# Two hybrid decoder layers on one core: the order of issue taken from the scheduler's time-line simulator

## The chip, the cores and the metric

The kernel runs on one core of one Trainium2 chip. The metric is the device time of one execution in microseconds. Every time below comes from one profiled execution of the kernel before, unless it is called a median of runs. The engines are TensorE (PE; PEld is its loading of weights), VectorE (DVE), ScalarE (ACT), GpSimd (POOL) and SyncE (SP); SP issues the DMAs.

## The reference, cut to what matters

One sequence of 256 rows of 2048 numbers goes through two layers. Each layer has an attention part (eight forgetting heads and eight differential heads) and an MLP part (hidden width 8192), and both are modulated by vectors that come from the condition `c` through the large matrix `w_ada` (2048 by 12288 for each layer).

```python
c_act = jax.nn.silu(c)
for l in range(DEPTH):                                   # 2 layers
    mod = c_act @ w_ada[l] + b_ada[l]
    sh_a, sc_a, g_a, sh_m, sc_m, g_m = jnp.split(mod[:, None, :], 6, axis=-1)
    h = x * (1.0 + sc_a) + sh_a
    y = _mixer(h, cos, sin, w_in[l], b_f[l], ..., w_o[l], _lambda_init(l))
    x = _layernorm(ALPHA * x + (1.0 + g_a) * y, ln1_g[l], ln1_b[l])
    h = x * (1.0 + sc_m) + sh_m
    y = jnp.square(jax.nn.relu(h @ w_up[l])) @ w_down[l]
    x = _layernorm(ALPHA * x + (1.0 + g_m) * y, ln2_g[l], ln2_b[l])
return x
```

All weights are float32: 768 blocks of 512 KB for the projections and 384 blocks of 512 KB for `w_ada`.

## The kernel before, in words

**One projection block.** A block is a 128x1024 piece of a weight matrix. SP loads it into a tile `raw` (L141). ACT copies it to `wh`, its rounded high part (L135), and DVE subtracts to get `wl`, the low part (L136). PE then multiplies in three products, high by high, high by low and low by high, with the activations `hT`, which were split in the same way (L485 is the high part, L486 the low part). A block is 12 matmuls of 128x512 (L302 to L304, in `mm3`) or 24 of 128x256 (L328 to L331, in `proj_T`). There are 7 buffers for `raw`, and 3 each for `wh` and `wl`: PE can be at most three blocks behind ACT and DVE.

**The modulation.** The product of `c` with `w_ada` is done on DVE. SP loads a block `rawa` (L156) into the same 7 buffers that `raw` uses, and DVE adds the block, times one column of `c`, to `acc` (L147 for the first block, L149 for the 15 that follow). Sixteen blocks make one piece of a modulation vector: PE transposes `acc` (L166), DVE reduces it (L171) and adds the bias `badaT` (L125, L173). ACT and DVE make `hT` from it (L483 to L486). For the two gates, the `acc` that comes out is split like a weight (its `wh` and `wl` take two of the projection's buffers) and goes through PE once with a matrix of ones (L201, L202).

**Stages.** The first layer's input projection is done in four passes over a quarter of the input columns each, since a pass can start as soon as its quarter of the modulation is there: piece 0 before the first matmul, the others beside the matmuls of the pass before. The passes end at about 96, 156, 215 and 300 us. The heads (softmax L597, gather of the gate biases `FR` L846), the output projection (`w_o`, added to the rows `xacc` at L495 to L498), a layer norm (statistics L502 to L506, normalized at L511, transposed at L470, its scale and shift applied later at L545 and L546 with the rows `gb` and `bb`) and the MLP follow, and then the second layer.

**What sets the order.** Every engine executes its instructions in a fixed order and waits at the first that isn't ready. The program is written with an interleaving of its own: `block` is called for each weight block and, by counters, mixes in blocks of `w_ada` (`side`), steps of the heads (`tasks`), and pieces of the layer norm's scale and shift (`later`); the numbers AHEAD, HOLDS, WAIT, GAP, LATER, PREP, STEP and RATES at its head set how much comes when. The layer in which the kernel is written takes the program and orders the instructions of every engine and the DMAs with a scheduler, which simulates the program as it goes; buffers are given out along that simulated run, and waits follow from it. In the listings, names carry a number: `rawa_1045` is the buffer that the program asked for as its 1045th object, and `wl_1004` is the low part made from `raw_1001` and `wh_1003`.

## Time and profile before

| what | value |
|---|---|
| median of 3 runs | 2357.38 us (2354.28 to 2359.78) |
| the profiled execution | 2353.96 us |
| its span in the profile | 2352.2 us |
| PE busy, share of the span | 2278.0 us, 97% |
| PE's weight loads (PEld) | 1958.9 us, 83% |
| DVE busy | 1791.8 us, 76% |
| ACT busy | 1156.4 us, 49% |
| moved by DMA | 619.36 MB, mean 263 GB/s |

The span is the time between the first and the last event of the profile; 1.8 us of the execution lie around it. A share of busy time is a mean over the whole span. A row of the time line tells the start, the duration, the engine, the line and the operation, and in brackets how long the engine stood idle just before and what ended this.

### The profile page before, as it was taken

What the parts mean: (1) busy time and instruction counts of PE and PEld (TensorE: products, weight loads), DVE (VectorE), ACT (ScalarE), POOL (GpSimd) and SP (SyncE); (2) the same over time, 40 slices, a digit from 0 to 9 for tenths busy, and PEclk for the clock granted to TensorE, in tenths of its full rate; (3) what the DMA queues carried; (4) which work ended last, traced back from release to release, by engine and by line L of the source; (5) the groups of instructions that cost most, each with busy time, mean ns of one, the idle gap of its engine ahead of it and who ended that gap; (6) DMA issues with size and microseconds to landing.
All of it is one profiled execution on the core that took longest, in us unless ns stands there. A gap on an engine that the chain in (4) does not pass through costs nothing.

```text
span 2352.2 us, 33293 instructions
## 1 busy us (share of the span) xinstructions
PE 2278.0 (97%) x12444; PEld 1958.9 (83%) x12444; DVE 1791.8 (76%) x2339; ACT 1156.4 (49%) x1684; POOL 35.1 (1%) x60
## 2 busy tenths in 40 slices
PE   4999999899999999999999999999999999999998
PEld 3878798799989888888877779987888888888886
DVE  7899988989888777888777975777675666555657
ACT  3544675345546345346444664544544643643542
POOL 0000010000000000000000000000000000000000
PEclk9999999999999999999999999999999999999999
DMA  9998578888898888888759867764687677655553
GB/s 341 329 331 310 199 272 307 316 313 327 303 351 299 307 283 305 316 285 307 274 189 314 293 225 243 254 206 169 226 271 242 232 243 240 229 194 190 186 189 123
DMA packets 174978, 619.36 MB, mean 263 GB/s; under 512 B 20105, under 2 KB 21209, under 8 KB 174817
## 3 DMA queue, kind: packets, MB, share of 16 engines
q1 hardware_dynamic: 174816, 617.25, 75.5%
q8 instruction: 97, 1.59, 0.3%
q14 instruction: 65, 0.52, 0.1%
HBM read 615.07 MB, written 2.10 MB: 262 GB/s over the span
## 4 chain that ended last, share of the span: by engine, by line
PE 85%; DVE 7%; DMA 4%; issue 2%; ACT 2%; POOL 0%; SPq 0%; DVEq 0%; ACTq 0%; POOLq 0%
PE mm L303 15%; PE mm L302 15%; PE mm L304 15%; PE mm L907 7%; PE bank L907 7%; PE mm L331 5%; PE mm L330 5%; PE mm L328 5%; PE mm L909 4%; PE bank L909 4%; DVE wl L136 2%; DVE acc L149 2%; DMA raw<-in_w_in_dram 1%; DMA rawa<-in_w_ada_G_dram 1%; DMA rawa<-in_w_ada_T_dram 1%
## 5 line engine op out<-in xcount | busy, mean ns | idle before, releaser
L135 ACT CAST wh<-raw 128x1024 fp32r<-128x1024 f32 x752 | 789.9, 1051 | 920.6 <-PE mm L304 489.7
L136 DVE TENSOR_TENSOR wl<-raw,wh 128x1024 fp32r<-128x1024 f32 x752 | 914.8, 1222 | 350.4 <-ACT wh L135 348.1
L149 DVE SCALAR_TENSOR_TENSOR acc<-rawa,cact,acc 128x1024 f32<-128x1024 f32 x368 | 471.2, 1280 | 118.8 <-DMA rawa<-in_w_ada_T_dram 66.8
L303 PE MATMUL mm<-wl,Hs 128*128 128x512 f32 x992 | 386.1, 389 | 1.0 <-DVE wl L136 1.0
L302 PE MATMUL mm<-wh,Hs 128*128 128x512 f32 x992 | 386.2, 389 | 0.0
L304 PE MATMUL mm<-wh,Hs 128*128 128x512 f32 x992 | 386.0, 389 | 0.0
L328 PE MATMUL mm<-hT,wh 128*128 128x256 f32 x1024 | 290.3, 284 | 1.9 <-DVE hT L485 1.1
L331 PE MATMUL mm<-hT,wl 128*128 128x256 f32 x1024 | 288.6, 284 | 2.9 <-DVE wl L136 2.4
L330 PE MATMUL mm<-hT,wh 128*128 128x256 f32 x1024 | 289.1, 283 | 0.2 <-DVE hT L486 0.2
L907 PE MATMUL mm<-hT,wh 128*128 128x512 f32 x768 | 287.1, 396 | 0.5 <-DVE hT L486 0.5
L907 PE MATMUL bank<-hT,wh 128*128 128x512 f32 x768 | 286.5, 395 | 0.0
L303 PEld LDWEIGHTS mm<-wl,Hs 128*128 128x128 f32 x992 | 186.2, 188 | 39.7 <-DVE wl L136 1.4
L302 PEld LDWEIGHTS mm<-wh,Hs 128*128 128x128 f32 x992 | 186.2, 188 | 38.8
L304 PEld LDWEIGHTS mm<-wh,Hs 128*128 128x128 f32 x992 | 186.2, 188 | 38.6
L909 PE MATMUL mm<-hT,wl 128*128 128x256 f32 x768 | 215.7, 281 | 0.1
L909 PE MATMUL bank<-hT,wl 128*128 128x256 f32 x768 | 215.4, 280 | 0.0
L302 PE MATMUL mm<-wh,hT 128*128 128x512 f32 x512 | 201.2, 400 | 5.7 <-DVE hT L485 5.7
L303 PE MATMUL mm<-wl,hT 128*128 128x512 f32 x512 | 203.5, 398 | 1.2 <-DVE wl L136 1.0
L304 PE MATMUL mm<-wh,hT 128*128 128x512 f32 x512 | 200.8, 393 | 0.0
L331 PEld LDWEIGHTS mm<-hT,wl 128*128 128x128 f32 x1024 | 195.3, 192 | 5.0 <-DVE wl L136 4.6
L328 PEld LDWEIGHTS mm<-hT,wh 128*128 128x128 f32 x1024 | 196.3, 192 | 3.4 <-DVE hT L485 1.3
L330 PEld LDWEIGHTS mm<-hT,wh 128*128 128x128 f32 x1024 | 196.3, 192 | 0.7 <-DVE hT L486 0.4
(248 smaller groups left out, 2666.6 us busy)
## 6 DMA issues: line engine op xcount, KB each, us to landing
rawa<-in_w_ada_T_dram SPq DMA_DIRECT2D x256, 512.0 KB, 5.2
raw<-in_w_up_dram SPq DMA_DIRECT2D x256, 512.0 KB, 4.7
raw<-in_w_down_dram SPq DMA_DIRECT2D x256, 512.0 KB, 4.5
raw<-in_w_in_dram SPq DMA_DIRECT2D x192, 512.0 KB, 4.8
rawa<-in_w_ada_G_dram SPq DMA_DIRECT2D x128, 512.0 KB, 5.0
raw<-in_w_o_dram SPq DMA_DIRECT2D x64, 512.0 KB, 4.6
gb<-in_ln_g_dram SPq DMA_DIRECT2D x12, 256.0 KB, 5.7
bb<-in_ln_b_dram SPq DMA_DIRECT2D x12, 256.0 KB, 5.2
```

The source lines that it names most:

```text
L135: nc.scalar.copy(wh, raw)
L136: nc.vector.tensor_sub(wl, raw, wh.bitcast(F32))
L149: nc.vector.scalar_tensor_tensor(acc, raw, k, acc, ALU.mult, ALU.add)
L302: nc.tensor.matmul(o, lhsT=hi, rhs=wh, start=start, stop=False)
L303: nc.tensor.matmul(o, lhsT=hi, rhs=wl, start=False, stop=False)
L304: nc.tensor.matmul(o, lhsT=lo, rhs=wh, start=False, stop=stop)
L328: nc.tensor.matmul(o, lhsT=wh[:, j, cs], rhs=hT[:, kt, 0, :], start=first and kt == kt0 and f % 2 == 0, stop=False)
L330: nc.tensor.matmul(o, lhsT=wh[:, j, cs], rhs=hT[:, kt, 1, :], start=False, stop=False)
L331: nc.tensor.matmul(o, lhsT=wl[:, j, cs], rhs=hT[:, kt, 0, :], start=False, stop=last and kt == kt1 - 1 and f % 2 == 1)
L907: nc.tensor.matmul(pu[f], lhsT=wh[:, j, cs], rhs=hT[:, kt].rearrange("p a s -> p (a s)"), start=kt == kt0, stop=False)
L909: nc.tensor.matmul(pu[f][:, 0:S], lhsT=wl[:, j, cs], rhs=hT[:, kt, 0, :], start=False, stop=kt == kt1 - 1)
```

## The change

One line of `kernel` changes:

```diff
-    with tile.TileContext(nc) as tc:
+    with tile.TileContext(nc, schedule_with_timeline_sim=True) as tc:
```

The scheduler has two simulators by which it orders the program. The other one, which is used now, follows a time line of engines and DMA queues. No instruction is added or taken away, none has another shape, and no count of buffers changes: each engine has the same work in another order, and the waits follow from that order. Three places show the kind of move.

On SP's queue at the start of the program (`-` before, `+` after; `xacc` are rows of the input, `pos_i`, `r`, `bfb`, `ta`, `tb` and `subg` are small constants):

```order
 L121 DMA r_119<-in_b_ada_dram 96x128
-L156 DMA rawa<-in_w_ada_T_dram 128x1024 x13
-L141 DMA raw<-in_w_in_dram 128x1024
+L156 DMA rawa<-in_w_ada_T_dram 128x1024 x5
+L1014 DMA xacc<-in_x_dram 128x512
+L156 DMA rawa<-in_w_ada_T_dram 128x1024
+L1014 DMA xacc<-in_x_dram 128x512
+L396 DMA pos_i<-in_positions_dram 128x2x1
+L156 DMA rawa<-in_w_ada_T_dram 128x1024
+L429 DMA r_518<-in_ln_g_dram 32x128
+L429 DMA r_518<-in_ln_b_dram 32x128
+L429 DMA r_518<-in_ln_g_dram 32x128
```

The list goes on in this way until the 16th `rawa`: all six remaining loads of input rows (256 KB each) and 12 loads of constants now stand ahead of or between the first 16 blocks of `w_ada`, where before all of them came later, spread over the passes.

On DVE at the start of the second pass, the kernel before:

```order
L485 CAST hT_102<-h32_806 128x2x256
L486 TENSOR_TENSOR hT_102<-h32_806,hT_102 128x2x256
L485 CAST hT_102<-h32_816 128x2x256
L486 TENSOR_TENSOR hT_102<-h32_816,hT_102 128x2x256
L136 TENSOR_TENSOR wl_876<-raw_873,wh_875 128x1024
L149 SCALAR_TENSOR_TENSOR acc_854<-rawa_906,cact_82,acc_854 128x1024
L136 TENSOR_TENSOR wl_912<-raw_909,wh_911 128x1024
L149 SCALAR_TENSOR_TENSOR acc_854<-rawa_939,cact_82,acc_854 128x1024
L136 TENSOR_TENSOR wl_945<-raw_942,wh_944 128x1024
L149 SCALAR_TENSOR_TENSOR acc_854<-rawa_977,cact_82,acc_854 128x1024
L136 TENSOR_TENSOR wl_983<-raw_980,wh_982 128x1024
L149 SCALAR_TENSOR_TENSOR acc_854<-rawa_998,cact_82,acc_854 128x1024
```

and the changed kernel:

```order
L136 TENSOR_TENSOR wl_912<-raw_909,wh_911 128x1024
L149 SCALAR_TENSOR_TENSOR acc_854<-rawa_939,cact_82,acc_854 128x1024
L485 CAST hT_102<-h32_806 128x2x256
L485 CAST hT_102<-h32_816 128x2x256
L149 SCALAR_TENSOR_TENSOR acc_854<-rawa_977,cact_82,acc_854 128x1024
L486 TENSOR_TENSOR hT_102<-h32_806,hT_102 128x2x256
L486 TENSOR_TENSOR hT_102<-h32_816,hT_102 128x2x256
L149 SCALAR_TENSOR_TENSOR acc_854<-rawa_998,cact_82,acc_854 128x1024
L149 SCALAR_TENSOR_TENSOR acc_854<-rawa_1023,cact_82,acc_854 128x1024
L149 SCALAR_TENSOR_TENSOR acc_854<-rawa_1045,cact_82,acc_854 128x1024
L149 SCALAR_TENSOR_TENSOR acc_854<-rawa_1070,cact_82,acc_854 128x1024
L136 TENSOR_TENSOR wl_945<-raw_942,wh_944 128x1024
```

Blocks 873 and 909 are now split before `hT` is made, and five `acc` steps stand ahead of `wl_945`, where before `wl` and `acc` took turns. In the changed order the load of `rawa_1045` waits for the `acc` step of `rawa_977`, and the load of `rawa_1070` for that of `rawa_1023`, because they get the buffers that these set free.

On DVE in the attention of the first layer, between two weight splits of the output projection, the kernel before:

```order
L136 TENSOR_TENSOR wl_3818<-raw_3815,wh_3817 128x1024
L149 SCALAR_TENSOR_TENSOR acc_3841<-rawa_3911,cact_82,acc_3841 128x1024
L597 ISA s_3791,mn_3792<-bank_3786,mask_89 128x128
L597 ISA mn_3792 128x1
L597 ISA s_3799,mn_3800<-bank_3786,mask_89 128x256
L597 ISA mn_3800 128x1
L136 TENSOR_TENSOR wl_3848<-raw_3845,wh_3847 128x1024
```

and the changed kernel, the first 12 of the 26 rows from the one split to the other:

```order
L136 TENSOR_TENSOR wl_3818<-raw_3815,wh_3817 128x1024
L597 ISA s_3030,mn_3031<-bank_3025,mask_89 128x128
L597 ISA mn_3031 128x1
L597 ISA s_3039,mn_3040<-bank_3024,mask_89 128x128
L597 ISA mn_3040 128x1
L597 ISA s_3047,mn_3048<-bank_3025,mask_89 128x256
L597 ISA mn_3048 128x1
L597 ISA s_3056,mn_3057<-bank_3024,mask_89 128x256
L597 ISA mn_3057 128x1
L846 TENSOR_TENSOR FR_3742<-FG_93,sel_91 128x1024
L149 SCALAR_TENSOR_TENSOR acc_3841<-rawa_3964,cact_82,acc_3841 128x1024
L680 SCALAR_TENSOR_TENSOR MXd_2161<-bank_3151,subg_99,MXd_2161 128x256
```

The softmax rows have lower numbers than the weights beside them: on every engine the weight blocks of the output projection now run ahead of the heads that the program had put before them. In the same way the 16 steps of the first layer norm's scale and shift (L545, L546), with the eight loads of `gb` and `bb`, now stand between `wl_6492` and `wl_6654` (about 622 to 640 us of the profile before) where they stood spread over 673 to 705 us; and on PE the matmuls of one gate half (L201, L202, the first layer's attention gate, half 0) come after 17 blocks that they stood ahead of, so that the gate's `wh` and `wl` are held all that time.

## Rows read from the trace of the kernel before

**Rows 1.** The page's first part: busy time, share of the span, instructions.

```profile
PE 2278.0 (97%) x12444; PEld 1958.9 (83%) x12444; DVE 1791.8 (76%) x2339; ACT 1156.4 (49%) x1684; POOL 35.1 (1%) x60
```

**Rows 2.** PE's waits: operation, what it waited for, total us, times, longest.

```profile
PE bank L166 <- DVE acc L149: 18.4, 1, 18.4
PE bank L470 <- DVE xacc L511: 15.0, 4, 6.9
PE bank L123 <- DMA r<-in_b_ada_dram: 8.0, 1, 8.0
PE mm L302 <- DVE hT L485: 5.7, 3, 3.4
PE mm L303 <- DVE wl L136: 3.1, 4, 1.0
```

**Rows 3.** Groups of the page: line, operation, count, busy us, mean ns, idle before.

```profile
L136 DVE TENSOR_TENSOR wl<-raw,wh 128x1024 fp32r<-128x1024 f32 x752 | 914.8, 1222 | 350.4 <-ACT wh L135 348.1
L149 DVE SCALAR_TENSOR_TENSOR acc<-rawa,cact,acc 128x1024 f32<-128x1024 f32 x368 | 471.2, 1280 | 118.8 <-DMA rawa<-in_w_ada_T_dram 66.8
```

**Rows 4.** Time line of the start: start us, us, engine, line, operation.

```profile
4.16 18.09 SPq L156 DMA_DIRECT2D rawa<-in_w_ada_T_dram  x13
...
11.19 0.26 DVE L125 COPY badaT<-bank 128x96 f32<-128x96 f32 x1 [5.61 <-PE bank L123]
11.37 19.77 DVE L149 SCALAR_TENSOR_TENSOR acc<-rawa,cact,acc 128x1024 f32<-128x1024 f32 x15
...
36.67 0.80 PE L302 MATMUL mm<-wh,hT 128*128 128x512 f32 x1 [3.45 <-DVE hT L485]
```

**Rows 5.** Stretches: us, busy PE, PEld, DVE, ACT, POOL, PE's clock, DMA share, GB/s.

```profile
0.00:36.00 36.00, 4.33 (x18) 3.48 (x18) 23.98 (x25) 5.58 (x8) 4.08 (x28) 1.00 0.95 362
96.00:156.00 60.00, 58.53 (x306) 48.87 (x304) 53.95 (x58) 26.47 (x32) 0.00 (x0) 1.00 0.91 330
464.50:474.50 10.00, 5.36 (x25) 4.97 (x25) 8.72 (x18) 1.93 (x4) 3.04 (x2) 0.50 0.57 189
620.00:640.00 20.00, 20.00 (x90) 16.57 (x89) 15.71 (x15) 10.31 (x13) 0.00 (x0) 1.00 0.90 303
673.00:706.00 33.00, 33.00 (x147) 27.36 (x146) 30.42 (x35) 14.18 (x15) 0.00 (x0) 1.00 0.97 353
1205.00:1208.00 3.00, 3.00 (x16) 2.91 (x15) 2.60 (x7) 2.80 (x7) 0.00 (x0) 0.53 0.00 0
```

**Rows 6.** DMA issues: operation, count, KB each, median us from issue to landing.

```profile
rawa<-in_w_ada_T_dram SPq DMA_DIRECT2D x256, 512.0 KB, 5.2
```

**Rows 7.** SP's time line, second pass: the load of `rawa_1045`.

```profile
105.80 0.33 SPq L156 DMA_DIRECT2D rawa<-in_w_ada_T_dram  x1
```

**Rows 8.** DVE's time line there: `wl_912`, `wl_945`, and the `acc` of `rawa_1045`.

```profile
101.16 1.22 DVE L136 TENSOR_TENSOR wl<-raw,wh 128x1024 fp32r<-128x1024 f32 x1
...
104.55 1.23 DVE L136 TENSOR_TENSOR wl<-raw,wh 128x1024 fp32r<-128x1024 f32 x1 [0.98 <-ACT wh L135]
...
115.74 1.28 DVE L149 SCALAR_TENSOR_TENSOR acc<-rawa,cact,acc 128x1024 f32<-128x1024 f32 x1
```

**Rows 9.** SP's time line in the second layer's input projection: one load.

```profile
1443.64 0.33 SPq L156 DMA_DIRECT2D rawa<-in_w_ada_T_dram  x1
```

**Rows 10.** DVE's time line there: two `acc` steps with their waits.

```profile
1447.70 1.28 DVE L149 SCALAR_TENSOR_TENSOR acc<-rawa,cact,acc 128x1024 f32<-128x1024 f32 x1 [1.81 <-DMA rawa<-in_w_ada_T_dram]
...
1453.39 1.28 DVE L149 SCALAR_TENSOR_TENSOR acc<-rawa,cact,acc 128x1024 f32<-128x1024 f32 x1 [1.81 <-DMA rawa<-in_w_ada_T_dram]
```

**Rows 11.** PE's time line in the output projection: first matmuls of two successive blocks.

```profile
401.39 0.39 PE L302 MATMUL mm<-wh,MXf 128*128 128x512 f32 x1
...
404.11 0.39 PE L302 MATMUL mm<-wh,MXf 128*128 128x512 f32 x1
```

**Rows 12.** DVE's time line: the split of the first block of rows 11.

```profile
396.13 1.23 DVE L136 TENSOR_TENSOR wl<-raw,wh 128x1024 fp32r<-128x1024 f32 x1
```

**Rows 13.** PE's time line: the wait in the norm after the first layer's MLP.

```profile
1204.62 3.16 PE L470 MATMUL bank<-ident,xacc 128*128 128x128 f32 x16 [3.56 <-DVE xacc L511]
```

## The prediction

> **What bounds the kernel now.** I read the busy shares first: PE is busy 97% of the span, DVE 76%, ACT 49% [rows 1]. Then PE's waits: all of them that are longer than a microsecond or two lie at the start (18.4 us for the first `acc`, 8.0 us for the bias, 3.4 of the 5.7 us for `hT`) and in the norms (15.0 us, of which 6.9 in one); for a weight split PE waited only 3.1 us in the whole program [rows 2]. So nearly everywhere PE is the bound, and ACT and DVE run ahead of it. How far ahead decides what a new order may cost. A block of 12 matmuls takes PE 404.11 - 401.39 = 2.72 us [rows 11]; its split ended at 396.13 + 1.23 = 397.36 us, 4.0 us before use [rows 11, 12]. With three buffers this lead cannot be much over two blocks, 5.4 us. DVE spends 1.22 us on a split and 1.28 us on an `acc` step [rows 3]: a pass with one `acc` step a block costs it 2.5 us in 2.72. There (96 to 156 us) PE is busy 58.53 of 60 us, DVE 53.95, and the DMA share is 0.91 [rows 5]. The opening has three resources near their limit, and the order there was the hand-made one. The matmuls' number and shapes stay, so I take their 2278 us as fixed, and ask at each place that the new order changes whether PE waits more or less.
>
> **The start, +6 us.** Six loads of 256 KB of input rows and 12 of constants (0.39 MB together) now go ahead of the 16th block of `w_ada`: 1.57 + 0.39 = 1.96 MB. At the 362 GB/s of this stretch [rows 5] that is 5.4 us. Before, the 15 `acc` steps ran without a gap, 19.77 us from 11.37 on [rows 4], so the last block had landed early. By bytes, 16 blocks of 0.524 MB and 0.57 MB of other loads take 24.7 us at that rate, from about 2 us on: landed at about 27, used at about 30. Of the 5.4 us, 3 are hidden by this, and the last `acc` ends 2.5 us later. Two `acc` steps now stand before the copy of `badaT`, which uses 2.6 of the 5.61 us that DVE waited there [rows 4], but this helps only if the blocks are there, and they are not. Behind the last `acc`, DVE has in its path to the first `hT` an `acc` step, another split and another `acc` step that stood behind it: 0.75 + 1.22 + 1.28 = 3.3 us (0.75 is the short first step; the others from [rows 3]). Sum 5.8. The other way, by bytes alone: 21 blocks must land before that last step, which with the rest is 13.5 MB, 37.3 us from 2 us on; the step, the cast and the first matmul follow at about 42, against 36.67 [rows 4], +5.5 at least. I take +6, from 2.5 (only the bytes, if the other steps find gaps) to 7.
>
> **The second pass, +5 us.** Between `wl_912` and `wl_945` DVE had one `acc` step; `wl_945` ended 105.78 - 102.38 = 3.4 us after `wl_912` [rows 8]. Now five `acc` steps and four `hT` steps stand there, and two of the `acc` steps use blocks whose loads wait for `acc` steps of the same group. From the end of `wl_912`: `acc`, two casts, `acc` 3.3 us; load 5.2 us [rows 6] to 8.5; meanwhile `acc` 998 and 1023 end at 7.0, which lets the second load land at 12.2; its `acc` 13.4, `wl_945` 14.6. Before, `rawa_1045` was issued at 105.80 and used at 115.74, almost 10 us later [rows 7, 8], and no latency showed. PE has blocks 824, 873 and 909 to do in that time, 8.2 us, but starts them only when the low part of `hT` is there, at 4.0: it runs dry at 12.2 and waits 2.4 us. `hT` itself comes later than it did: an `acc`, a split and another `acc` (3.8 us) stand between the modulation and its cast, where a short first `acc`, a split and a copy stood (2.2 us), and an `acc` between high and low part adds 1.2. Together 2.4 + 1.6 + 1.2 = 5.2. I take +5, from 4 to 6.
>
> **Passes two to four otherwise, +4 us.** DVE's order now uses `rawa` blocks three to five places earlier than SP's order loads them, so a slot that is freed is wanted again within two or three DVE steps. Two rows price this from both sides. In the second layer the old order had that too: a block issued at 1443.64 was used at 1447.70, after DVE had waited 1.81 us for it, and 5.7 us later the same again [rows 9, 10]; PE was not held there, because only every other block had an `acc` step. That is 0. In the opening every block has one. Then a period is the load's latency and the steps behind it, some 3.3 to 3.9 us, where PE takes 2.72: 0.6 to 1.2 us for each of some 15 blocks less the lead, up to +12. The first row is the nearer one in kind, and the second stretch the nearer one in DVE's load; I take +4.
>
> **Attention of layer 0, +4 us.** Two splits now have long stretches of other work ahead of them: `wl_3848`, with softmax of two heads, `FR` and two `acc` steps (6.8 us of other work by the mean times of these operations, then another 2.0 before `wl_3896`), and `wl_4267`, behind all of a gated addition and its statistics (8.4 us). With the splits themselves PE sees its next low part 11.2 and 9.6 us after the one before, and has 5.3 and 3.0 us of work in between. The lead of 4.0 us [rows 11, 12] leaves 1.9 and 2.6 us, one of 5.4 leaves 0.5 and 1.2, one of 3 leaves 2.9 and 3.6. So 2 to 6.5; I take +4. The gate that holds a `wh` and a `wl` during 17 blocks leaves two buffers, which cuts the lead, but DVE's work is light there; with PE at no wait for splits I put it into these bounds.
>
> **The norms' scale and shift, +2 and +1 us.** Sixteen steps of 0.69 us, spaced 0.6, move from a stretch where DVE had 30.42 of 33 us into one where it had 15.71 of 20 and the DMA share was 0.90 [rows 5]. For the seven blocks there DVE now needs 23.1 us (9.6 for these steps, 8.5 for the splits, 5 for `acc`), PE 19.0: the lead of 4.0 just covers it, half of it leaves 2; and 2.1 MB of rows in a stretch with a tenth of the queue free may hold `raw` up to 2 more: +2, from 0 to 4. At the second layer's start the sixteen steps of the other norm come closer together in the same way, 20.5 us of DVE against 16.3 of PE in six blocks: +1, from 0 to 2. The start of the first MLP has `rawa` blocks in the order of the opening, at one step to a block or fewer: +1, from 0 to 5.
>
> **The norms, -1 us.** Around the norms the splits of the next blocks now stand before the norm's steps, and those run back to back. PE waited 15.0 us here in four waits [rows 2]; the chain from the last matmul through statistics and normalizing to `hT` stays, so I give back 1 us, at most 2.
>
> Sum: 6 + 5 + 4 + 4 + 2 + 1 + 1 - 1 = +22 us on the profiled execution's 2353.96, which is 2376. It lay 3.4 us under the median of the runs, 2357.38; for a median I say **2379 us**.
>
> **Rivals.**
> *The opening falls to the pace of its loads.* If the period of 3.3 to 3.9 us holds through the passes, the third term is +12 and the start of the MLP +5: +34, and with the upper ends of the other terms +45: 2391 to 2402. For it: DMA share 0.91 and DVE 53.95 of 60 [rows 5]. Against: 1.96 MB less is to be loaded in those passes now.
> *PE's clock.* After the wait of 6.9 us [rows 2] the granted clock was 0.50 in the 10 us from 464.5 on [rows 5], which is the lower level, 1.2 GHz; that cost 5 us. If two or three of the new waits are as long as the shortest one with such an effect, 3.56 us [rows 13], behind which the clock was 0.53 for 3 us [rows 5], each costs 1.5 to 5 us more: +5 to +10, 2384 to 2389. The Trainium skill says so in "TensorE: Matmul & The Clock Gate", section "HAM oscillation — how this bites in real kernels": waits for transfers between bursts of matmuls throw the clock back, and each burst then starts cold. By that rule the opening would pay at every block, but the clock is 1.00 in 96 to 156 us with its waits of about 1 us [rows 5], so the trace bears it out for long waits only.
> *Nothing to measure.* The three-deep buffers take it all but part of the start, and the norms give 2 us back: within 4.7 us of 2357.
> *Faster.* The norms hold 15.0 us of waits [rows 2] and about 5 us of lower clock. If the back-to-back norm steps took away half, -10, and start and opening cost no more than +4, the time would be 2351. The point is whether the first normalize after each layer part is issued 2 us or more earlier behind the last matmul. Against it: the order cannot shorten the chain, and the start alone costs more than 4 by bytes. The Trainium skill, "Perfetto Trace Analysis", section "Identifying the Most-Contended Engine", holds that matmul busy time says little about headroom and that weight-load time should be read, which is 83% here; by that there would be more than 3% to gain. But blocks follow each other at 2.72 us with no gap that an order could close [rows 11].
>
> **How the numbers follow.** Forecast (+10 to +33 us) 0.66; loads' pace 0.10; clock on top of the forecast 0.07 (most of it in the forecast's upper part); a small loss of 5 to 10 us 0.04; nothing to measure 0.07; faster 0.06. A measurement of this kernel can tell about 0.2%, 4.7 us. The range goes from +5 us, 2362, to +45, 2402; it leaves out the last two cases and a little above. Slower 0.87, same 0.07, faster 0.06.
>
> **What would show it.** Right: the first weight matmul at 42 to 44 us; a wait of PE of several us near 115 to 125 us for `wl`; the clock at 1.00 in the passes; PE waits for `wl` of some 10 us in all instead of 3.1; one or two waits between 370 and 430 us; one of 1 to 4 us near 640 us; PE's busy time unchanged within a few us. Wrong: a first matmul before 39 us, or passes of 60 us or less; then the buffers hide more than I count. If PE's busy time grows by more than 10 us, it was the clock.

## The result: 57 us slower, more than the range held

| what | before | after |
|---|---|---|
| median, 4 runs each on one chip | 2357.53 us | 2414.66 us |
| lowest and highest | 2354.28 to 2359.78 | 2409.69 to 2421.33 |
| profiled execution | 2353.96 us | 2409.69 us |
| ratio after to before | | 1.0245 (95% interval 1.0229 to 1.0261) |

The sign of the forecast was right, its size was not: +22 us was forecast, at most +45 were allowed for, and the measured change is +57.

### The profile page after: what moved, and what is told of

Its sections match the earlier page's. It is cut to its first block, busy times and chain, and to the rows that moved or that the text cites. A ratio compares the mean times of both kernels' runs of the same rounds, so it can differ in the third digit from the quotient of the medians.

```text
span 2407.9 us, 33303 instructions
## 1 busy us (share of the span) xinstructions
PE 2290.7 (95%) x12444; PEld 1958.3 (81%) x12444; DVE 1784.5 (74%) x2339; ACT 1161.3 (48%) x1684; POOL 31.6 (1%) x60
## 4 chain that ended last, share of the span: by engine, by line
PE 62%; DMA 17%; DVE 14%; issue 5%; ACT 1%; SPq 0%; DVEq 0%; POOL 0%; ACTq 0%; POOLq 0%
DMA rawa<-in_w_ada_T_dram 11%; PE mm L303 11%; PE mm L304 11%; PE mm L302 11%; PE mm L907 6%; PE bank L907 6%; DVE wl L136 6%; DVE acc L149 4%; DMA rawa<-in_w_ada_G_dram 3%; PE mm L909 3%; PE bank L909 3%; PE mm L331 3%; PE mm L330 3%; PE mm L328 3%; DMA raw<-in_w_o_dram 1%
## 5 line engine op out<-in xcount | busy, mean ns | idle before, releaser
L149 DVE SCALAR_TENSOR_TENSOR acc<-rawa,cact,acc 128x1024 f32<-128x1024 f32 x368 | 472.0, 1283 | 246.1 <-DMA rawa<-in_w_ada_T_dram 155.7
L304 PE MATMUL mm<-wh,Hs 128*128 128x512 f32 x992 | 387.1, 390 | 0.0
L302 PE MATMUL mm<-wh,Hs 128*128 128x512 f32 x992 | 347.5, 390 | 0.0
L331 PE MATMUL mm<-hT,wl 128*128 128x256 f32 x1024 | 285.3, 287 | 5.9 <-DVE wl L136 5.7
L907 PE MATMUL bank<-hT,wh 128*128 128x512 f32 x768 | 281.2, 396 | 0.0
L907 PE MATMUL mm<-hT,wh 128*128 128x512 f32 x768 | 277.3, 397 | 0.0
L303 PE MATMUL mm<-wl,hT 128*128 128x512 f32 x512 | 204.7, 400 | 10.7 <-DVE wl L136 10.5
L909 PE MATMUL bank<-hT,wl 128*128 128x256 f32 x768 | 207.3, 281 | 0.0
L909 PE MATMUL mm<-hT,wl 128*128 128x256 f32 x768 | 201.9, 281 | 4.9 <-DVE wl L136 4.9
L331 PEld LDWEIGHTS mm<-hT,wl 128*128 128x128 f32 x1024 | 193.7, 193 | 10.0 <-DVE wl L136 8.6
L304 PE MATMUL mm<-wh,hT 128*128 128x512 f32 x512 | 199.4, 391 | 0.0
L302 PE MATMUL mm<-wh,hT 128*128 128x512 f32 x512 | 186.0, 396 | 8.5 <-DVE hT L485 6.1
```

The lines of the kernel that those rows point to most:

```text
L149: nc.vector.scalar_tensor_tensor(acc, raw, k, acc, ALU.mult, ALU.add)
L302: nc.tensor.matmul(o, lhsT=hi, rhs=wh, start=start, stop=False)
L303: nc.tensor.matmul(o, lhsT=hi, rhs=wl, start=False, stop=False)
L304: nc.tensor.matmul(o, lhsT=lo, rhs=wh, start=False, stop=stop)
L331: nc.tensor.matmul(o, lhsT=wl[:, j, cs], rhs=hT[:, kt, 0, :], start=False, stop=last and kt == kt1 - 1 and f % 2 == 1)
L907: nc.tensor.matmul(pu[f], lhsT=wh[:, j, cs], rhs=hT[:, kt].rearrange("p a s -> p (a s)"), start=kt == kt0, stop=False)
```

## The profile after

The page of the changed kernel, its first part and the shares of the chain that ended last:

```profile
span 2407.9 us, 33303 instructions
...
PE 2290.7 (95%) x12444; PEld 1958.3 (81%) x12444; DVE 1784.5 (74%) x2339; ACT 1161.3 (48%) x1684; POOL 31.6 (1%) x60
...
PE 62%; DMA 17%; DVE 14%; issue 5%; ACT 1%; SPq 0%; DVEq 0%; POOL 0%; ACTq 0%; POOLq 0%
...
L149 DVE SCALAR_TENSOR_TENSOR acc<-rawa,cact,acc 128x1024 f32<-128x1024 f32 x368 | 472.0, 1283 | 246.1 <-DMA rawa<-in_w_ada_T_dram 155.7
```

Every engine's count of instructions is that of [rows 1], and DVE's 368 `acc` steps still last 1.28 us each [rows 3]. New is what lies in front of them: DVE stood idle 246.1 us before these steps instead of 118.8, and 155.7 us of that for the transposed blocks of `w_ada` instead of 66.8 [rows 3]. The chain shows the same from the other end: in the kernel before, 85% of its length was PE, 7% DVE and 4% DMA; now 62% is PE and 17% DMA. So this view points at an answer before any experiment: DVE waits for blocks that it adds, and PE waits behind DVE. The experiments below test it.

PE's waits in the changed kernel (what waited, for what, total us, times, longest):

```profile
PE bank L166 <- DVE acc L149: 25.4, 1, 25.4
PE mm L303 <- DVE wl L136: 22.7, 32, 2.5
PE bank L470 <- DVE xacc L511: 15.3, 3, 8.2
...
PE mm L302 <- DVE hT L485: 6.1, 1, 6.1
PE mm L331 <- DVE wl L136: 5.7, 11, 1.5
PE mm L909 <- DVE wl L136: 4.9, 6, 1.5
PE mm L302 <- ACT wh L135: 3.2, 2, 1.8
PE mm L328 <- DVE hT L485: 3.0, 1, 3.0
```

In the kernel before, the same list has a second row for a low part, which [rows 2] doesn't show:

```profile
PE mm L331 <- DVE wl L136: 2.4, 3, 1.7
```

Against [rows 2] and this row: the wait for the first `acc` grew by 7.0 us, the norms' waits stayed (15.3 us, 15.0 before), and the waits for a low part went from 3.1 + 2.4 = 5.5 us in seven waits to 22.7 + 5.7 + 4.9 = 33.3 us in 49, the longest 2.5. No one place is bad; PE runs dry again and again, for 0.7 us on average. PE's busy time grew by 12.7 us too. By the last test of the prediction that would be its clock, and for the most part it is not: the stretches at half clock sum to 32.4 us, 26.1 before, which costs 3 us. A matmul's record is longer (0.39 us) than the distance to the next (0.23 us), so a stall shorter than the difference looks like busy time. Where time was lost is therefore read below from a ledger and not from the listed waits alone.

**The ledger.** Each weight block has the same name in all these kernels, so the end of its last matmul can be compared with the kernel before. The delay at the ends of seven stretches (named by the time in the trace of before) gives what each stretch lost. Where heads and weight blocks have changed places, as inside the first attention, single blocks say nothing; the ends of the stretches lie where both orders have done the same work. Columns are the changed kernel and the experiments of the next sections; from run to run a stretch that is the same in two kernels differs by 1 to 3 us. The start, for one, costs 10.0 to 12.0 us in the runs that keep the changed order there.

| stretch (us of before) | after | e1 | e2 | e3 | e4 | e8 | e10 | e11 |
|---|---|---|---|---|---|---|---|---|
| start, to 41.8 | 10.0 | 7.5 | -1.0 | 10.3 | -1.0 | 11.5 | 11.7 | 0.0 |
| passes, to 254.6 | 5.9 | 2.9 | -6.1 | 31.6 | 0.8 | 7.8 | 5.6 | 0.1 |
| attention 0, to 440.6 | 14.0 | 9.1 | 16.0 | 16.9 | 10.6 | 0.7 | 14.2 | 2.4 |
| norm, first blocks of MLP 0, to 766.8 | 3.7 | 8.9 | 5.2 | 12.0 | 8.5 | 4.9 | 8.5 | 1.2 |
| rest of MLP 0, to 1187.0 | 15.4 | 3.0 | 14.7 | 4.2 | 2.7 | 15.7 | 3.3 | -2.4 |
| layer 1, start, to 1278.2 | 5.4 | 6.1 | 3.8 | 21.0 | 0.6 | 5.7 | 3.7 | 0.7 |
| rest, to 2341.0 | 1.7 | 12.1 | 8.4 | 24.7 | 15.1 | 3.0 | 9.1 | 2.8 |
| all | 56.1 | 49.6 | 41.0 | 120.7 | 37.3 | 49.3 | 56.1 | 4.8 |

Four rows carry the loss: the start, the passes, the first attention, and the first MLP beside which the gates and the second layer's modulation are computed. The last of these has 15.4 us and had no term in the sum.

## The experiments

**How an order is held.** All the experiments use one function. It adds, between successive instructions of a list, an edge for the scheduler that demands this order and puts no wait into the program. A list holds one engine's instructions, in the order that they have in the kernel before unless something else is said. The function is called behind the whole program; each experiment has its own lists.

```diff
+def held_order(tc, nc):
+    traced = {i.name: i for i in nc.cur_bb.bb.instructions}
+    for steps in ORDERS:
+        at, last = 0, None
+        for step in steps.split():
+            at += int(step)
+            ins = traced["I-%d" % at]
+            if last is not None:
+                tc.add_manual_dep(ins, last.name, mybir.DependencyInfo(mybir.DependencyClass.NoSync,
+                                                                       mybir.DependencyReason.DATA),
+                                  reason="held order")
+            last = ins
...
         decoder(tc, *args)
+        held_order(tc, nc)
```

This has a limit, which a comparison of the orders instruction by instruction shows: the scheduler arranges the engines that are not held around those that are. With only DVE held (e1), PE's instructions in the first attention stand on average 3 places from the kernel before, where in the changed kernel they stand 84 places from it. With only SP held (e2), DVE's order in the passes is 2 places from the kernel before and 10 from the changed one. So "one engine's order alone" is true of the engine that is named and not of the others, and the text says at each place which of them had stayed.

### Is it the order at all, and whose?

Edits: e11 holds all four engines (PE, DVE, ACT, SP) through the whole program and is otherwise the changed kernel; e1 to e4 hold DVE, SP, PE, and DVE with SP. The lists of e4, cut:

```diff
+ORDERS = ["""86 2 22 14 -11 3 53 3 3 3 3 3 3 3 3 3 3 3 3 12 22
...
+"""74 35 3 3 2 1 2 48 3 3 3 3 3 3 3 3 3 3 3 3 31 17 1
...
     with tile.TileContext(nc, schedule_with_timeline_sim=True) as tc:
```

> The time-line simulator, with PE, DVE, ACT and SP all held in the order of the kernel before; what it still decides is which buffer goes to which tile, and GpSimd's order. If the order of issue is the whole of the cause: 2352 to 2362. If the buffers and the waits that follow from them carry a part: over 2365.

Measured: 2358.76 us, with the kernel before at 2356.93 on that chip. The changed line with the old orders takes the old kernel's time: GpSimd, which was not held, and the giving out of buffers have no part in the loss that stands out of the spread (the kernel before took 2351 to 2361 us on that chip). The order of the four engines is the cause.

> The changed kernel with DVE held in the order that it has in the kernel before; all other engines are ordered by the time-line simulator. By the blocks' end times the changed kernel loses 10 us at the start, 7 in the passes, 14 in the attention of layer 0, 15 in the MLP of layer 0, 5 at the start of layer 1 and 9 in its attention (of which 9 are gained back there by the order of heads). Theory D, the order on DVE is the cause (acc steps and softmax ahead of splits): the losses behind the start go and the start keeps most of its 10, about 2368 us. Theory L, the order in which SP loads and the buffers are given out is the cause: little changes, 2395 or more. Theory P, the order on PE (gates late, blocks ahead of heads) is the cause: the passes and the MLP recover 10 to 20, the attention does not, about 2390.

> The changed kernel with SP's loads held in the order of the kernel before, DVE, ACT and PE by the time-line simulator. Theory D: only the start recovers, first weight matmul at 38 to 40 us instead of 46.2, total about 2405. Theory L: the passes and the MLP recover too, 2375 or less. Theory P: as theory D.

> The changed kernel with PE held in the order of the kernel before, DVE, ACT and SP by the time-line simulator. Theory D: start, passes and MLP keep their losses, the attention too or more of it: 2405 to 2420. Theory P: the attention of both layers recovers its 14 and 9 us: 2390 or less. Theory L: as theory D.

> The changed kernel with both DVE and SP held in the order of the kernel before, ACT and PE by the time-line simulator. Theories D and L both expect the kernel before within 10 us (2355 to 2367); first weight matmul at 37 us. Theory P: the attention's losses of 14 and 9 us remain, 2375 to 2385.

Measured, with the kernel before at 2361.72 us: e1 2403.16, e2 2394.58, e3 2474.40, e4 2390.80. None comes back, and PE's old order makes it 60 us worse than no order held. By their totals none of the three theories holds: e3 and e4 fit none, e2 lies between them, and e1 alone is where theory L had put it. Two of the reasons are visible: these mixtures hold PE up long enough that it spends more time at half clock (58.2 us in e1, 54.5 in e4 and 119.6 in e3, against 26.1 before), and orders that don't fit each other wait for each other. PE's longest waits in e3:

```profile
PE bank L166 <- DVE acc L149: 26.5, 1, 26.5
PE bank L737 <- DVE lf L733: 25.6, 2, 17.1
...
PE mm L302 <- DVE hT L485: 12.7, 3, 6.3
```

The waits at L737 belong to the heads: PE takes these up at their old place, and DVE, which is 7 places from its old order there, isn't done. Totals of such mixtures say little, so I read them by stretch. SP's old order takes away the loss of the start (e2 and e4: -1.0); DVE's old order takes away that of the MLP (e1 3.0, e4 2.7); in the first attention both leave 9 to 16 us. SP's order has no part in that stretch: there it is the same in both kernels.

### The start: which loads cost what

Edits, on the kernel before with all four orders held as they were: e5 moves the six loads of input rows ahead as the changed kernel does, and nothing else; e6 the 12 loads of constants; e16 issues the constants on ACT's queue instead of SP's, early too: at 5 to 16 us, where the changed kernel issues them at 11 to 27 us and e6 at 13 to 24.

The first line is SP's list as it was, then those of e5 and e6:

```diff
-"""74 35 3 3 2 1 2 48 3 3 3 3 3 3 3 3 3 3 3 3 31 17 1
+"""74 35 3 3 2 1 2 48 3 3 3 3 72 -69 70 -67 3 3 3 626
...
+"""74 35 3 3 2 1 2 48 3 3 3 3 3 283 -280 333 26 22 27
```

and the edit of e16, two of six places:

```diff
-            nc.sync.dma_start(r2[i * 32:(i + 1) * 32], v.rearrange("l (a p) -> (l a) p", p=P))
+            nc.scalar.dma_start(r2[i * 32:(i + 1) * 32], v.rearrange("l (a p) -> (l a) p", p=P))
...
-        nc.sync.dma_start(bfb, b_f.rearrange("(o l) n -> o l n", o=1).broadcast_to([P, DEPTH, NF]))
+        nc.scalar.dma_start(bfb, b_f.rearrange("(o l) n -> o l n", o=1).broadcast_to([P, DEPTH, NF]))
```

> The kernel before with all engines held in its own order, but with the six loads of input rows at the places on SP that the changed kernel gives them. Theory B (bytes: 1.57 MB ahead of the last rawa block): first weight matmul 1.5 to 4.5 us later than 36.67, and about as much in total. Theory Q (SP's queue: small loads hold up the issue of rawa): at most 1.5 us later.

> The kernel before with all engines held in its own order, but with the 12 loads of constants (0.39 MB) at the places on SP that the changed kernel gives them. Theory B: first weight matmul 0 to 1 us later than 36.67. Theory Q: 4 to 7 us later, since in the changed kernel SP issued five such loads 1.3 us apart and the next rawa only at 19.34 us.

> The kernel before with its engines held, and the 12 loads of constants issued early as in the changed kernel, but from ACT's queue instead of SP's. With them on SP the first weight matmul was at 39.80 us, 3.1 late. If the price is SP's place in line (its issue waits, with rawa behind): 36.5 to 37.5 us. If it is the transfers themselves: 39 or more.

Measured by the first weight matmul, which is at 36.67 us in the kernel before [rows 4]: e5 37.93, +1.3; e6 39.80, +3.1; e16 39.68, +3.0. (Their times, 2355.43, 2358.81 and 2360.81 us beside 2354.55, 2354.55 and 2359.90, are too near the measurement's 4.7 us.) The 0.39 MB of constants cost more than twice what the 1.57 MB of rows cost. Theory B, the bytes, has that the wrong way round, and theory Q, the queue of SP, asked for 4 us or more from the constants. In the time line of the changed kernel SP issues five of them between two blocks of `w_ada`, for 5 us, and the last `acc` step and the first matmuls follow late:

```profile
14.04 0.33 SPq L429 DMA_DIRECT2D r<-in_ln_g_dram  x1
...
18.59 0.35 SPq L434 DMA_DIRECT2D bfb<-in_b_f_dram  x1
19.34 0.35 SPq L156 DMA_DIRECT2D rawa<-in_w_ada_T_dram  x1
...
36.34 1.28 DVE L149 SCALAR_TENSOR_TENSOR acc<-rawa,cact,acc 128x1024 f32<-128x1024 f32 x1 [1.32 <-DMA rawa<-in_w_ada_T_dram]
37.77 1.94 PE L166 MATMUL bank<-ident,acc 128*128 128x128 f32 x8 [25.37 <-DVE acc L149]
46.17 0.80 PE L302 MATMUL mm<-wh,hT 128*128 128x512 f32 x1 [6.07 <-DVE hT L485]
```

What they do to the stream around them is in the stretches from 12 to 20 and 20 to 28 us. The columns are start and end, length, busy PE, PEld, DVE, ACT, POOL, PE's clock, DMA share, GB/s. First the changed kernel from 20 us:

```profile
20.00:28.00 8.00, 0.00 (x0) 0.00 (x0) 4.89 (x20) 0.00 (x0) 0.00 (x0) 1.00 0.81 248
```

e5, rows early:

```profile
20.00:28.00 8.00, 0.00 (x0) 0.00 (x0) 7.50 (x7) 0.00 (x0) 0.00 (x0) 1.00 1.03 403
```

e6, constants early:

```profile
20.00:28.00 8.00, 0.00 (x0) 0.00 (x0) 5.44 (x5) 0.00 (x0) 0.00 (x0) 1.00 0.82 277
```

e16, constants early on ACT's queue, from 12 us:

```profile
12.00:20.00 8.00, 0.78 (x4) 0.38 (x2) 6.99 (x6) 1.15 (x2) 0.00 (x0) 1.00 0.71 217
```

The kernel before moves 410 and 402 GB/s in these stretches. Rows leave that as it is; constants take it to 277 for 8 us, which is 8 x (402 - 277) = 1.0 MB that did not come, 2.5 us at 402 GB/s, and more from 12 to 20 us (352 instead of 410, 1.2 us). That is 3.7 us of the stream on top of the 1.1 that the bytes of 0.39 MB alone ask for. It isn't SP's place in line: with SP freed of the constants (e16) the dip is as large, 1.5 MB, and only comes 8 us earlier, as they are issued earlier, and the first matmul is at the same time. Why they cost so much is shown in part: in e6's trace from 12 to 30 us they are about 1500 packets of 4 to 512 bytes, which took 29 us of the 16 DMA engines' time, so 1.8 us of the stream. The rest is DMA engines that stood idle (a share of 0.82 in the row of e6, 1.02 in the kernel before) and packets of the large loads that took 175 ns instead of 163; why, no run shows. The Trainium skill says in "DMA: Bandwidth & Descriptors", section "Issuing engines are not separate DMA queues", that transfers issued by any engine run on the same 16 DMA engines and interleave; 39.68 against 39.80 us agrees with it.

The two parts don't add up singly. As an estimate: if the lead that the blocks had hides 3 us (the prediction's figure) of either alone and of both together only once, rows are 1.3 + 3 = 4.3, constants 3.1 + 3 = 6.1, and both together 4.3 + 6.1 - 3 = 7.4 us. e1, with DVE's old order and SP left free, has 7.5 us there. The rest up to the 10.0 us is put down to DVE's new order, 2.5 us (up to 4.5 by the runs with 12.0); in the trace, the way from the last `acc` to the first matmul grew by 3.0.

### The passes

The prediction followed one chain in the second pass through DVE's new order. DVE's time line of the changed kernel there (`wl_912`, ..., the `acc` of `rawa_1045` and `rawa_1070`, `wl_945`):

```profile
105.21 1.22 DVE L136 TENSOR_TENSOR wl<-raw,wh 128x1024 fp32r<-128x1024 f32 x1
...
114.64 1.28 DVE L149 SCALAR_TENSOR_TENSOR acc<-rawa,cact,acc 128x1024 f32<-128x1024 f32 x1 [1.26 <-DMA rawa<-in_w_ada_T_dram]
118.00 1.29 DVE L149 SCALAR_TENSOR_TENSOR acc<-rawa,cact,acc 128x1024 f32<-128x1024 f32 x1 [2.07 <-DMA rawa<-in_w_ada_T_dram]
119.20 2.36 DVE L136 TENSOR_TENSOR wl<-raw,wh 128x1024 fp32r<-128x1024 f32 x2
```

`wl_945` ends 119.20 + 1.22 - 106.43 = 14.0 us after `wl_912`; 14.6 were predicted, and 3.4 it was before [rows 8]. The wait of PE that should follow isn't at this block, though. PE's own time line has it earlier, at `hT`:

```profile
108.01 1.22 PE L328 MATMUL mm<-hT,wh 128*128 128x256 f32 x4 [3.01 <-DVE hT L485]
```

(In the kernel before, the waits at this place are 1.05 us, and 0.23 for the low part of `hT`; here they are 3.01 and 0.91.) The stretch behind it (columns as above) shows why PE then came late enough to block 942:

```profile
107.80:114.60 6.80, 5.68 (x25) 5.38 (x26) 5.37 (x7) 0.07 (x1) 0.00 (x0) 0.50 0.91 321
```

After 3.0 us of waiting the granted clock was 0.50, the 1.2 GHz level, for 6.8 us, which costs half of the 5.68 us that PE was busy in them, 2.8; PE asked for `wl_945` at 120.3 and had it at 120.4. The place cost what was predicted (2.6 for `hT`, 2.8 for the clock; 5.2 had been said), and a clock drop took the place of a wait. e7 (see the first MLP), where no `acc` step of the pass waits for its load, loses 5.4 us here too, by the same wait and the same drop, and 5.4 over all the passes, with `wl_945` ready in time. So by this run the loss of the passes isn't made by waits for blocks of `w_ada`.

### The first attention

Edits: from 235 to 455 us (of the kernel before) e8 holds all four engines, e13 all but DVE, e14 all but PE, e15 all but ACT. e9 holds a single pair, the gate's first matmul ahead of the first matmul of the weight block that it stood before.

The lists of e8 are, in this order, PE's, DVE's, ACT's and SP's; e13, e14 and e15 leave out the second, the first and the third:

```diff
+ORDERS = ["""2067 1 1 1 1 1 1 1 1 1 1 24 1 1 1 1 1 1 1 1 1 1
...
+"""2044 34 -32 6 27 100 -130 35 -34 35 -34 35 -33 1 1 1
...
+"""2045 139 -136 155 -86 134 -81 6 136 48 -123 6 184
...
+"""2309 45 3 64 3 35 3 117 22 3 140 3 34 8 124 3 37 112
```

and e9:

```diff
+ORDERS = ["""2907 14"""]
```

> The changed kernel with all four engines held in the order of the kernel before for those instructions that lie between 235 and 455 us there (attention and output projection of layer 0). If the order in this stage is what costs its 14 us: the blocks' delay at the stage's end is 16 to 20 us instead of 30, total 2398 to 2404. If the loss comes in from the stages before it (late loads): it stays at 27 or more.

> As the run with the attention of layer 0 held on all four engines (which lost nothing there, 19.3 to 20.0 us between 254 and 440 us), but with DVE left to the time-line simulator. If DVE's order in the stage is what costs the 14 us: a loss of 10 or more between 254 and 440 us. If it is PE's or ACT's order: 3 or less.

> The same with PE left to the time-line simulator, DVE, ACT and SP held in the stage. If PE's order (blocks ahead of the heads, gate late) costs the 14 us by itself: 10 or more between 254 and 440 us; if it needs DVE's order too: 4 or less.

> The same with ACT left to the time-line simulator, PE, DVE and SP held in the stage. Neither theory puts the loss on ACT: 4 or less between 254 and 440 us. 8 or more would put it on the copies to wh that stand behind the heads' softmax.

> The changed kernel with one ordering edge: PE's matmuls of the gate half that 17 blocks overtake (L201, L202) come before the second block that had overtaken them, as in the kernel before; the rest is ordered by the time-line simulator around it. If the two buffers that the gate holds are a main cause of the attention's 14 us: the blocks' delay at 440 us is 22 to 26 us instead of 30, total 2400 to 2409. If not (splits behind softmax, late heads): 28 to 32, total 2410 to 2417.

| kernel | time (before on its chip) | lost in 254.6 to 440.6 | free engine's places from before |
|---|---|---|---|
| after | 2409.69 (2353.96) | 14.0 | PE 84, DVE 32, ACT 19 |
| e8 | 2402.89 (2354.55) | 0.7 | |
| e15 | 2410.96 (2359.90) | 1.3 | ACT 0.5 |
| e14 | 2415.52 (2359.90) | 5.0 | PE 3 |
| e13 | 2447.34 (2359.90) | 26.9 | DVE 6 |
| e9 | 2426.07 (2356.93) | 13.5 | PE 56, DVE 23, ACT 11 |

e8 settles that the loss in this stretch is made by the orders in it, and that none of it is inherited from the late start. PE's waits while this stretch ran (what, for what, total, times, longest) tell the two apart. The changed kernel has fifteen of them from 270 to 470 us of its own time, 10.9 us in all, of which the first two rows are:

```profile
PE mm L303 <- DVE wl L136: 3.5, 4, 1.4
PE mm L302 <- ACT wh L135: 3.2, 2, 1.8
```

e8 has seven, 3.1 us in all (274 to 461 us), most of them at the heads:

```profile
PE bank L647 <- ACT pT L611: 1.3, 3, 0.6
PE mm L328 <- ACT wh L135: 0.9, 1, 0.9
...
PE mm L303 <- DVE wl L136: 0.3, 1, 0.3
```

What e13 to e15 don't settle is how the 14 us divide among the engines. The free engine was put near its old place in each, not at its place in the changed kernel, and a DVE order that is only six places off cost more (26.9 us) than the whole new arrangement, in which all engines were moved together. Its largest waits, from 270 to 500 us of its own time:

```profile
PE bank L737 <- DVE lf L733: 9.0, 1, 9.0
PE bank L607 <- DVE s L656: 3.4, 1, 3.4
PE bank L607 <- ACT s L629: 2.5, 1, 2.5
```

The stretch is 285 to 498 us there, so the first of these, which ended at 270.7, isn't in the 26.9: it and a clock drop are in the row of the passes, where e13 lost 19.2 us. About 10 of the 26.9 are the clock, which stood at 0.50 for 20 us. So DVE's order has to fit PE's here, and a share for each engine isn't to be had from these runs. Of ACT's new order e15 says nothing, since ACT stood half a place from its old one. The gate by itself isn't the cause: e9 gives it back its place and loses 13.5.

The two splits that the prediction named do wait. `wl_3896` ended 10.7 us after `wl_3818` (11.2 predicted), and PE lost 1.8 us at its block (by the record for the high part, which ACT makes) and 1.4 at a split among the steps of the gated addition, the place of `wl_4267`: together 3.2 us, where 4 were predicted. Beside them are others of 0.4 to 1.4 us, for splits and high parts of blocks with no such pile ahead of them and for steps of the heads.

### The first MLP

Edits: e10 holds DVE alone, from 700 to 1190 us of the kernel before. e7 keeps the changed kernel's orders on all engines and lets the `acc` steps read another tile, so that none waits for its load; e17 does the same with the orders of the kernel before.

e10:

```diff
+ORDERS = ["""7177 -27 32 2 -1 2 6 57 -27 33 71 -27 31 -49 92
```

e7 and e17:

```diff
+    steps = [0]
...
     def ada_add(acc, raw, kt, fresh):
         k = cact[:, kt:kt + 1]
+        steps[0] += 1
+        if steps[0] > 16 and not fresh:
+            raw = acc
```

> The changed kernel with DVE alone held in the order of the kernel before, and only for instructions that lie between 700 and 1195 us there (MLP of layer 0). If DVE's order makes the MLP's loss (acc steps ahead of splits, waiting for their loads): the 15 us there become 0 to 4, total 2397 to 2404. If PE's or SP's order makes it: 10 or more remain, total 2408 or more.

> The changed kernel with all engines held in its own order, but the steps L149 behind the first piece of the modulation read acc in place of their rawa block, so that they don't wait for its load; the loads stay. The modulation is wrong, which leaves the amount of work as it is. Theory W (splits stand behind acc steps that wait for their loads): the loss of 15 us in the MLP of layer 0 falls to 3 or less, the one in the passes to 4 or less, the start of layer 1 to 1; total 2380 to 2392. Theory O (DVE has too much other work in front of the splits, whatever it waits for): the MLP keeps 10 or more, total above 2400.

> The kernel before with all engines held in its own order, and the L149 steps behind the first piece of the modulation reading acc in place of their rawa block (the modulation is wrong, which leaves the amount of work as it is): the control of the run in which the changed kernel does the same. PE waits for splits only 3.1 us in the kernel before, so theory W expects a gain of 0 to 3 us; a gain of 8 or more would say that the waits for rawa cost the old order too.

DVE's time line of the changed kernel, in this stretch (start us, us, engine, line, operation, idle before and what ended it):

```profile
862.28 1.22 DVE L136 TENSOR_TENSOR wl<-raw,wh 128x1024 fp32r<-128x1024 f32 x1
864.55 1.28 DVE L149 SCALAR_TENSOR_TENSOR acc<-rawa,cact,acc 128x1024 f32<-128x1024 f32 x1 [1.05 <-DMA rawa<-in_w_ada_T_dram]
865.76 2.35 DVE L136 TENSOR_TENSOR wl<-raw,wh 128x1024 fp32r<-128x1024 f32 x2
869.67 1.29 DVE L149 SCALAR_TENSOR_TENSOR acc<-rawa,cact,acc 128x1024 f32<-128x1024 f32 x1 [1.56 <-DMA rawa<-in_w_ada_T_dram]
...
874.63 2.35 DVE L136 TENSOR_TENSOR wl<-raw,wh 128x1024 fp32r<-128x1024 f32 x2
879.86 1.28 DVE L149 SCALAR_TENSOR_TENSOR acc<-rawa,cact,acc 128x1024 f32<-128x1024 f32 x1 [2.88 <-DMA rawa<-in_w_ada_T_dram]
```

SP issued the blocks of the second and the last of these steps at 865.87 and 874.74, that is 3.8 and 5.1 us before their use. In the kernel before, the same two were issued 5.3 and 6.5 us before use and waited for by nobody. Over the whole stretch the median from issue to use fell from 6.1 us (94 blocks) to 5.2 (90), and a block takes about 5 to land [rows 6]; used in less than 5 us were 14 blocks before and 37 now, 10 in e10. SP's order is the same in both kernels here, place for place; DVE's steps are moved by two places on average, and that is enough: a step that stood behind a split stands ahead of it, finds its block not landed, and the split, which could have run, waits behind it. DVE's waits in this stretch (what, for what, total us, times, longest), first of the changed kernel, 770 to 1235 us:

```profile
DVE acc L149 <- DMA rawa<-in_w_ada_T_dram: 55.0, 39, 3.1
DVE acc L149 <- DMA rawa<-in_w_ada_G_dram: 25.7, 16, 3.6
DVE wl L136 <- ACT wh L135: 15.2, 17, 1.8
```

The same of e10:

```profile
DVE wl L136 <- ACT wh L135: 37.7, 33, 2.4
DVE acc L149 <- DMA rawa<-in_w_ada_T_dram: 23.3, 21, 3.5
...
DVE acc L149 <- DMA rawa<-in_w_ada_G_dram: 11.7, 10, 1.8
```

And of the kernel before, 725 to 1190 us:

```profile
DVE wl L136 <- ACT wh L135: 50.8, 58, 1.6
DVE acc L149 <- DMA rawa<-in_w_ada_T_dram: 16.6, 18, 3.6
DVE acc L149 <- DMA rawa<-in_w_ada_G_dram: 11.6, 11, 2.0
```

80.7 us of waiting for blocks instead of 28.2, and with DVE's old order 35.0. The first lines matter as much: before, DVE waited 50.8 us for high parts, which means that it was ahead of ACT and had no split left to do; in the changed kernel this reserve is down to 15.2 us, and what is missing beyond that is missing at PE: 52.5 us more of waiting less 35.6 of reserve is 16.9 us, beside the 15.4 that the stretch lost. PE's listed waits for a low part there are 1.0 us in the kernel before, 9.9 in the changed one and 5.6 in e10. In e10 the loss of the stretch is 3.3 us instead of 15.4, while PE and ACT kept the order of the changed kernel within a place. SP's order was the changed kernel's too. That is the cleanest of the partial runs, and e1 (3.0) and e4 (2.7) agree with it. So does e3, with 4.2: nobody held DVE there, but the scheduler put it 1.3 places from its old order in this stretch instead of 2.1.

Its total missed: 2409.64 us, nothing gained. Of the 12 us, 5 went at the seam, where DVE changes from one order to the other (695 to 767 us: 6.3 us lost, 1.4 in the changed kernel), and 7 from 1278 us on (9.1 instead of 1.7), nearly all of it in the second attention. So the cause of this stretch is shown, and what it is worth by itself in the total is not.

e7, 2395.27 us (before 2354.55), is in the same direction: without waits for blocks the stretch loses 0.1 us up to 907 us where the changed kernel loses 5.9, and the first attention 8.8 instead of 14.0, so that by this run about 5 us of that one are waits for `w_ada` blocks. Its total is above what theory W said, and the passes (5.4) and the start of layer 1 (2.8) lost more than that theory allowed. Past 907 us it fails as a probe: it loses 20 us by 1046 us, because loads for the projection come late instead and one step waits 8.4 us for a bias. e17, 2358.48 us (before 2354.66), shows the other side: in the old order these waits cost nothing, and taking them away gains nothing.

### A mixture that might have been better

In e2 the blocks of the third pass ended 4.4 us earlier than in the kernel before. e12 therefore holds all four engines in the order of e2 up to 205.5 us and in that of the kernel before from there on. The lists of PE and DVE, cut; the last two lines compare with the changed kernel:

```diff
+ORDERS = ["""81 41 36 1 1 1 2 1 1 1 41 1 1 1 2 1 1 1 25 1 2 1 43
...
+"""86 2 22 3 3 8 45 3 3 3 3 3 3 3 3 3 3 3 3 12 22 -21
...
-    with tile.TileContext(nc, schedule_with_timeline_sim=True) as tc:
+    with tile.TileContext(nc) as tc:
```

> The kernel before with all engines held: up to the third pass (what had started before 205.5 us) in the order of the run with only SP held, and from there on in its own order. If the 4.4 us that the blocks were early in that run by 177 us are kept to the end: 0.15 to 0.2% faster than the kernel before, 2352 to 2355. If the passes after it take them back: the same.

> The mix of two orders once more with more rounds, since its first comparison (0.999, interval 0.9979 to 1.0001) did not tell it from the kernel before: 0.998 to 1.000, 2352 to 2357 us.

e12: 2353.99 us, median of 10, against 2356.93, ratio 0.999 (0.9979 to 1.0001). e18, the same kernel on another chip: 2355.23, median of 11, against 2354.66, ratio 0.9999 (0.9988 to 1.0009). It isn't told from the kernel before. In e12's trace 4.6 us are there at 240 us of before and 2.4 are left at 441; two drops of the clock of 3.4 us each, near 272 and 292 us, lie in between. None of these kernels is measurably faster than the kernel before.

## Why the prediction was too low, point by point

**Bound and direction: right.** PE was the bound, the new order added waits (5.5 us for low parts became 33.3; the prediction read 3.1 for the 5.5, since [rows 2] leaves out the row of L331), and nothing came back: the norms' waits are 15.3 us against 15.0, where -1 was predicted. The rival "faster" needed half of these to go; they stayed to a third of a microsecond.

**The start: +10.0, predicted +6, at most 7.** The term was put together from a transfer part and a DVE part. The DVE part was 3.3 and measured 2.5 to 3.0 in this trace. The transfer part was 2.5 and is 7.0 to 7.5: the constants were priced by bytes, at 1.1 us, and took 3.7 us more of the stream than that. The first matmul is at 46.2 us; 42 to 44 was to be seen.

**The second pass and the passes: +5.9, predicted +5 and +4.** The chain through `wl_945` was right to 0.6 us in length, and the later `hT` cost 2.6 us where 2.8 were counted. The other half agrees in part by luck: the 2.4 us of waiting for `wl_945` weren't there, and a clock drop of 2.8 us that the term didn't have was. Without the drop PE would have come to `wl_945` that much earlier and might have waited for it; e7 shows only that the drop is enough by itself. The rest of the passes lost nearly nothing on top. Here the lower of the two bounds, the one of [rows 9, 10], held.

**The first attention: +14.0, predicted +4, at most 6.5.** The two places that were named cost about what was said. The step that failed was the selection: I looked for long piles of work ahead of a split and took the rest of a stretch, in which PE's order had moved by 84 places and DVE's by 32, as free of cost. e8 shows that the orders in the stretch cost 13 us more than the old ones; by e7 about 5 of these are waits for `w_ada` blocks, the waits at the named splits are 3.2 (the two can overlap), and the division of the rest among engines stays open.

**The first layer norm's scale and shift: +0.5 at 640 us, predicted +2; the start of layer 1: +5.4, predicted +1.** The first was counted too high. The second stretch had PE wait five times for a split, 5.1 us in all, with DVE's waits for `rawa` at 13.9 us instead of 9.0. That looks like the mechanism of the MLP again; no run was made for it alone, so it isn't shown.

**The first MLP: +15.4, predicted 0, with +1 at its start.** This is the step that put the time out of the range: it is the largest term and it was missing. Its mechanism wasn't: the rival "the opening falls to the pace of its loads" describes it, an `acc` step put ahead of a split and behind a load that has just been issued. I confined it to the opening and priced it at zero wherever only every other block has a step, from [rows 9, 10]: DVE waited 1.8 us there in the old order and PE did not notice. That reading was of single waits with a reserve behind them. The reserve is the DVE time spent waiting for high parts, 50.8 us in this stretch; the waits for blocks went from 29 to 55 there and used up 36 us of it, and where none was left PE waited. The order showed it as well: DVE's 426 rows in this MLP move by two places on average, and I read only the long moves.

**The clock: as far as it went.** One new wait of 3.0 us at 108 us was followed by 6.8 us at the lower level, as the rival said of longer waits (its shortest was 3.56 us). The 49 waits for a split, none over 2.5 us, were not, and the total at half clock grew by 6.3 us only. The rival's condition, a long wait, isn't the only one, though: in the kernel before the clock also stood at 0.50 for 3.4 us from 1341.7 us on, in the heads of the second layer, behind a listed wait of 0.9 us. PE's busy time rose by 12.7 us, of which the clock explains 3, so this sign in the list of what would show it was a bad one.

The sum with the terms as measured is 10 + 6 + 14 + 4 + 15 + 5 + 2 = 56 us. The two that fail most are the attention (10 us too low) and the MLP (15 us). The median of 2414.66 us lies 12.7 us above the range's end of 2402: with the MLP's 15.4 us counted at zero, as the prediction had it, the time would have been inside, and with the attention as predicted it would not.

## What to carry to other kernels

Where an engine both prepares operands and adds to something whose blocks have only just been requested, a shift by two places in its order can be enough: read from the trace the time from a block's load to its use, compare it with what a load takes, and count how many steps a new order pulls below that, however short the moves are. Look at the reserve of such an engine (its waits for an input that comes from ahead of it) by stage and not at single waits that were harmless. And orders belong together: here the old order of one engine, put among the new orders of the others, cost up to 60 us more than the new order of all (e3), and no partly held order brought the old time back.

## What the runs showed of the hardware that I had not expected

Twelve small constant loads of 0.39 MB in a stream of 512 KB blocks took the rate from 402 to 277 GB/s for 8 us, and to 217 GB/s, 8 us earlier, when they were issued on ACT's queue; six loads of 256 KB in the same place left it at 403. By bytes the constants are a fifth of both together, in time they are the larger part.
